# Small products of a token-mixing chain on four quarters of the matmul array, and a mean taken out of v beforehand

## The chip, the cores and the metric

The kernel runs on one core of a Trainium2 chip. The metric is device time in microseconds (us): the median of three runs, and beside it one execution taken by the hardware profiler. TensorE multiplies matrices, VectorE and ScalarE do elementwise work and copy results out of the accumulator memory (PSUM), GpSimd and SyncE mostly issue DMAs.

## The reference

A decoder trunk of two layers for one sequence of 512 tokens and 1,024 channels, in fp32. Each layer has three stages, each with an RMS norm, a shift, a scale and a gate made from a conditioning vector: a gated feed-forward net (width 2,816), a token mixing, and a second feed-forward net. The mixing projects the tokens to 20 tiles of 128 channels and runs three mixers on them: sliding-window attention with sinks, a short gated convolution, and the time mixing that this change is about:

```python
def step(S, inp):
    r_t, w_t, k_t, v_t, kk_t, a_t = inp
    s_kk = jnp.einsum('bhvk,bhk->bhv', S, kk_t)
    S = (S * w_t[:, :, None, :] - s_kk[..., None] * (kk_t * a_t)[:, :, None, :]
         + v_t[..., None] * k_t[:, :, None, :])
    return S, jnp.einsum('bhvk,bhk->bhv', S, r_t)
...
y = y - mean over the head;  y = y * rsqrt(var + eps) * gn_w + gn_b
```

It has four heads of 64 channels. Its decay w and its rate a come from low-rank products (64 inner channels each). y is linear in v, so the mean of y over a head's channels is zero when v's mean over them is taken out first.

## The kernel before, in words

All activations lie transposed: channels on the 128 partitions, the 512 tokens along the free dimension. Large products are done with each fp32 operand split into a rounded part H and a remainder L (`split`, L133 on ScalarE and L135 on VectorE), as three matmuls (`mm3`, L121 to L123). Feed-forward stages (`ffn`) stream weights and use the same three matmuls, at L420 to L422 for products of sums. Their moving operands are the normed activations hn (pools hnp and hnp2), combined halves com and hidden activations act (pool act). Pools are laid out one behind the other in on-chip memory; four tiles that are never used (shift, shift2, gap, gap2 of 448 and 64 bytes) move hnp, hnp2 and com against the rest.

`mix` (one call a layer) is written as Python generators that yield a cost. `products` emits the projection tiles and the first output products step by step; `attention` and two chains `rwkv(0)` and `rwkv(1)`, each for two heads, yield estimated costs. The loop at the end of `mix` emits product steps in proportion to those costs: RWKV_WORK, ATT_WORK and FILL_WORK are the totals, so a chain with a smaller total gets more product steps per unit of its cost. A scheduler then orders each engine's instructions; the order is fixed before the run, and an engine waits in it for what isn't ready.

A chain treats 512 tokens as 8 chunks of 64, that is 4 blocks b of two chunks c, and two heads e. Tiles [128, 2, 4, 64] hold chunk c on partition half c, with head e and block b along the free dimension. Its steps:

1. Low-rank products ps_w (L753) and ps_a (L755), contracting over the lower and the upper 64 partitions of lo and lw. lo has been through a tanh on ScalarE (L693).
2. Elementwise preparation on VectorE and ScalarE, with two reciprocals (L779, L780) and head sums by a block-of-ones matrix (`headsum`, L610).
3. `pairs` (L811): products of the chunks, ps_c, masked into B and K (L814).
4. The inverse of a unit triangular 64x64 matrix per chunk and head: its 16x16 diagonal blocks go through DRAM, are eliminated on VectorE (L839, L840) and come back as T and TT (L888, L889). Two levels of `each` (L897) join the blocks: ps_x, ps_t and ps_tt, with X (L902), T (L906) and TT (L909) taken out by one VectorE step of 512 columns each.
5. v, be and ka turned to token-major tiles by TensorE transposes (L853); values' share ps_xv (L874); W (ps_w2, L916; the profile names it ps_w), which multiplies TT into AX and is copied out negated (L917).
6. Per-chunk transfer ps_gn (L926 to L930), outputs ps_o (L942 to L946), six state steps ps_s (L954), their outputs ps_ys (L960).
7. Group norm: mean by `headsum` (ps_m), subtraction (L965), square, variance (ps_v), scale, bonus, gate (ps_g, L980).

A matmul takes its weights and moving operand from the partitions where they start and writes the partitions of its output, so an operand on 64 partitions and an output on 64 partitions use one quarter of the 128x128 array. In steps 4 and 5, chunk c reads partition half c and writes partition half c: two quarters on the diagonal. In ps_gn and ps_o, chunk c reads half c and head e writes half e, into one accumulator per c. Each chain owns two accumulator banks (tags r0 and r1).

## Time and profile before

| what | value |
|---|---|
| median of 3 runs | 1867.47 us (1863.78 to 1871.3) |
| the profiled execution | 1866.04 us, of which its span is 1864.0 |
| granted clock of TensorE | 0.994 |
| VectorE and ScalarE busy, share of the span | 75%, 45% |
| the two mixing stages | about 371 to 622 and 1285 to 1536 us of the span |

A group's row reads: line, engine, operation, output<-inputs, rows x columns of the array, shape, count; then busy us, mean ns of one; then idle time before it and what ended it. A timeline row reads: start, length, engine, line, operation, count of merged instructions. Matmuls overlap, so the distance between starts, and not the length of one, says how long a matmul holds the array. In the rows of waits stand the total, the number and the longest, in us.

### The profile page before, as it was taken

The page shows a single profiled execution, that of the slowest core. Times are in us where ns is not written, and L with a number is a line of the kernel's source. Part 1 is how long each engine was busy: PE and PEld are TensorE (multiplying, and loading weights), DVE is VectorE, ACT ScalarE, POOL GpSimd, SP SyncE. Part 2 cuts the span into 40 slices and gives each one's busy share as a digit, 9 for nine tenths or more (in the row PEclk, how much of TensorE's full clock was granted, in tenths as well). Part 3 has the DMA queues.
Part 4 walks back from the last instruction along what each step waited for, and adds up shares of the span by engine and source line. Part 5 has one row for each costly group of instructions (what it writes and reads, how often), then busy time and mean ns, then how long its engine had stood idle before and what let it go on. Part 6 is the DMA issues. An engine that isn't in the chain of part 4 may idle for free.

```text
span 1864.0 us, 33421 instructions
## 1 busy us (share of the span) xinstructions
PE 1828.7 (98%) x13664; PEld 1644.4 (88%) x13664; DVE 1398.4 (75%) x2202; ACT 836.3 (45%) x1272; POOL 130.9 (7%) x212
## 2 busy tenths in 40 slices
PE   8999999999999999999999999999999999999999
PEld 6889899986777999899999988999767788998998
DVE  7687677867986887777878786777589778874872
ACT  4443255346422555245345524544563335532551
POOL 0101110100000000110100020110000000100100
PEclk8999999999999999999999999999999999999999
DMA  7667876621122475886737688773212125775752
GB/s 307 225 185 234 263 197 202 221 83 46 58 55 72 136 195 176 296 223 195 246 112 197 171 272 228 192 229 114 101 56 59 53 68 161 209 227 139 203 144 68
DMA packets 104313, 308.24 MB, mean 165 GB/s; under 512 B 23392, under 2 KB 24416, under 8 KB 103136
## 3 DMA queue, kind: packets, MB, share of 16 engines
q1 hardware_dynamic: 75936, 203.34, 32.3%
q0 software_dynamic: 28224, 102.77, 21.7%
q8 instruction: 107, 1.75, 0.4%
q14 instruction: 46, 0.38, 0.1%
HBM read 302.66 MB, written 3.41 MB: 164 GB/s over the span
## 4 chain that ended last, share of the span: by engine, by line
PE 71%; DVE 13%; DMA 7%; issue 4%; ACT 4%; POOL 1%; SPq 0%; POOLq 0%; DVEq 0%; ACTq 0%
PE ps_mm L121 11%; PE ps_mm L122 10%; PE ps_mm L123 10%; PE ps_d L420 6%; PE ps_d L422 6%; PE ps_d L421 6%; PE ps_f L420 3%; PE ps_f L422 3%; PE ps_f L421 3%; DMA wada<-in_wadaT 2%; DVE wL L135 2%; PE ps_g L422 2%; PE ps_g L420 2%; PE ps_g L421 2%; ACT wH L133 1%
## 5 line engine op out<-in xcount | busy, mean ns | idle before, releaser
L133 ACT CAST wH<-wraw 128x1024 fp32r<-128x1024 f32 (+2 forms) x292 | 266.1, 918 | 434.7 <-PE ps_mm L122 190.2
L135 DVE TENSOR_TENSOR wL<-wraw,wH 128x1024 fp32r<-128x1024 f32 (+2 forms) x292 | 307.2, 1058 | 105.1 <-ACT wH L133 104.4
L123 PE MATMUL ps_mm<-actH,wL 128*128 128x512 f32 (+1 forms) x784 | 281.5, 359 | 2.8 <-DVE wL L135 2.8
L121 PE MATMUL ps_mm<-actH,wH 128*128 128x512 f32 (+1 forms) x784 | 281.6, 359 | 0.0
L122 PE MATMUL ps_mm<-actL,wH 128*128 128x512 f32 (+1 forms) x784 | 281.2, 359 | 0.0
L121 PE MATMUL ps_mm<-hnH,wH 128*128 128x512 f32 (+1 forms) x760 | 267.5, 359 | 5.7 <-ACT hnH L133 2.9
L122 PE MATMUL ps_mm<-hnL,wH 128*128 128x512 f32 (+1 forms) x760 | 266.5, 353 | 0.5
L123 PE MATMUL ps_mm<-hnH,wL 128*128 128x512 f32 (+1 forms) x760 | 266.4, 353 | 0.6 <-DVE wL L135 0.6
L420 PE MATMUL ps_d<-comH,wH 128*128 128x256 f32 x816 | 224.7, 275 | 0.3 <-ACT s L446 0.3
L421 PE MATMUL ps_d<-comL,wH 128*128 128x256 f32 x816 | 224.4, 275 | 0.0
L422 PE MATMUL ps_d<-comH,wL 128*128 128x256 f32 x816 | 224.4, 275 | 0.0
L192 DVE SCALAR_TENSOR_TENSOR wada<-wada,crep 128x1024 f32<-128x1024 f32 x140 | 167.7, 1219 | 48.8 <-DMA wada<-in_wadaT 48.2
L135 DVE TENSOR_TENSOR wL<-sum,wH 128x1024 fp32r<-128x1024 f32 x102 | 124.9, 1224 | 71.5 <-ACT wH L133 71.3
L123 PEld LDWEIGHTS ps_mm<-actH,wL 128*128 128x128 f32 x784 | 149.1, 190 | 20.3 <-DVE wL L135 3.6
L121 PEld LDWEIGHTS ps_mm<-hnH,wH 128*128 128x128 f32 x760 | 143.4, 191 | 24.9 <-issue 3.8
L121 PEld LDWEIGHTS ps_mm<-actH,wH 128*128 128x128 f32 x784 | 149.1, 190 | 16.8
L122 PEld LDWEIGHTS ps_mm<-actL,wH 128*128 128x128 f32 x784 | 149.0, 190 | 16.8
L123 PEld LDWEIGHTS ps_mm<-hnH,wL 128*128 128x128 f32 x760 | 145.5, 191 | 19.3 <-issue 4.3
L122 PEld LDWEIGHTS ps_mm<-hnL,wH 128*128 128x128 f32 x760 | 145.4, 192 | 17.2 <-DVE hnL L277 1.6
L420 PEld LDWEIGHTS ps_d<-comH,wH 128*128 128x128 f32 x816 | 156.7, 192 | 0.9 <-ACT s L446 0.9
L422 PEld LDWEIGHTS ps_d<-comH,wL 128*128 128x128 f32 x816 | 156.7, 192 | 0.0
L421 PEld LDWEIGHTS ps_d<-comL,wH 128*128 128x128 f32 x816 | 156.7, 192 | 0.0
(354 smaller groups left out, 3855.6 us busy)
## 6 DMA issues: line engine op xcount, KB each, us to landing
wada<-in_wadaT POOLq DMA_DIRECT2D x128, 512.0 KB, 4.8
wraw<-in_wmi SPq DMA_DIRECT2D x40, 512.0 KB
wraw<-in_w2p SPq DMA_DIRECT2D x36, 512.0 KB
wraw<-in_w1p SPq DMA_DIRECT2D x32, 512.0 KB
wraw<-in_w1o SPq DMA_DIRECT2D x32, 384.0 KB
wraw<-in_w2o SPq DMA_DIRECT2D x32, 384.0 KB
wraw<-in_w1i SPq DMA_DIRECT2D x20, 512.0 KB
wraw<-in_w1o SPq DMA_DIRECT2D x32, 320.0 KB
```

What stands on the lines that cost most here:

```text
L121: mm(acc, wH, xH, start=start, stop=False)
L122: mm(acc, wH, xL, start=False, stop=False)
L123: mm(acc, wL, xH, start=False, stop=stop)
L133: nc.scalar.copy(hi, src)
L135: return nc.vector.tensor_sub(lo, src, hi.bitcast(F32))
L192: stt(w, w, 1.0, crep, ALU.mult, ALU.mult, accum_out=out_)
L420: mm(acc, wH, xH, start=start and i + k == 0, stop=False, skip_group_check=True)
L421: mm(acc, wH, xL, start=False, stop=False, skip_group_check=True)
L422: mm(acc, wL, xH, start=False, stop=k == 3, skip_group_check=True)
```

## The change

- **Two quarters to four.** The products of the inverse, values' share and W write head 0's chunk c to partition half c of one accumulator (as before), and head 1's chunk c to half 1-c of a second. Each result is now copied out by three instructions: all of head 0, and the two halves of head 1, which change partition halves on the way. ps_t and ps_tt of the first level share a pair of accumulators; W is one block instead of two.
- **Low-rank products** are done in halves of 256 tokens, ps_w and ps_a in turn. They are ordered one behind the other across both chains, behind the tanh, and given high priority, so that all 16 follow each other.
- **Mean.** v is turned by a matmul against cen (identity minus the mean over a head) instead of a transpose. ps_m and its subtraction go. The bonus term uses the v that isn't centred. cen adds 128 columns (512 bytes a partition) to the constants.
- **Pads.** The four unused tiles go.
- **Order.** `pairs`, ps_gn and ps_o start with half 1 instead of half 0.
- **Planner.** The yields follow the shorter steps; RWKV_WORK is 24.3 instead of 29.8.

In the built programs each engine's order changes with it. On TensorE the 16 low-rank matmuls stand behind the second value product of attention's first block. Before the first chain's first ps_x stand 426 product matmuls of the stage (436 before) and 22 fewer of ps_c. VectorE's order has T ahead of both B steps, two convolution steps and a weight split, and ends the elimination ahead of the second reciprocal of the other chain.

```diff
-GAP = 448
-RWKV_WORK, ATT_WORK, FILL_WORK = 29.8, 15.2, 129.6
+RWKV_WORK, ATT_WORK, FILL_WORK = 24.3, 15.2, 129.6
...
-    ("ident", P), ("bones", P), ("bones2", 2), ("su", CH), ("iu", CH), ("diag", CH),
+    ("ident", P), ("bones", P), ("bones2", 2), ("cen", P), ("su", CH), ("iu", CH), ("diag", CH),
...
-    shift = ctx.enter_context(tc.tile_pool(name="shift", bufs=1))
-    shift.tile([P, GAP // 4], F32, name="shift")
     hnp = [ctx.enter_context(tc.tile_pool(name=n, bufs=KD)) for n in ("hnp", "hnp2")]
-    shift = ctx.enter_context(tc.tile_pool(name="shift2", bufs=1))
-    shift.tile([P, (512 - GAP) // 4], F32, name="shift2")
...
-            ap_.tile([P, GAP // 4], F32, name="gap", tag="gap")
-            ap_.tile([P, (512 - GAP) // 4], F32, name="gap2", tag="gap2")
...
-            act(got["lo"][:64], got["lo"][:64], AF.Tanh)
+            got["tanh"] = act(got["lo"][:64], got["lo"][:64], AF.Tanh)
...
             pw = psum([P, T], "ps_w", R)
-            mm(pw, lw[:64, cw], lo[:64], start=True, stop=True)
             pa = psum([P, T], "ps_a", R)
-            mm(pa, lw[64:, cw], lo[64:], start=True, stop=True)
-            yield 1.7
+            behind = got.get("lora", got["tanh"])
+            with tc.high_priority():
+                for sl in HALVES:
+                    for e, pt in enumerate((pw, pa)):
+                        m = mm(pt[:, sl], lw[rows[e], cw], lo[rows[e], sl], start=sl is HALVES[0], stop=sl is HALVES[1])
+                        tc.add_manual_dep(m.ins, behind.ins.name, ORDER, reason="halves of the rows run together")
+                        behind = got["lora"] = m
+            yield 1.2
...
-                        for e in range(2):
+                        for e in (1, 0):
                             mm(pts[e][rows[c], b], src[rows[e], n * CH : (n + 1) * CH], AR[rows[e], :, n], start=True, stop=True)
...
-                    nc.tensor.transpose(pt[:, b], src[:, b * P : (b + 1) * P], cst("ident"))
+                    x = src[:, b * P : (b + 1) * P]
+                    if name == "ps_vN":
+                        mm(pt[:, b], x, cst("cen"), start=True, stop=True)
+                    else:
+                        nc.tensor.transpose(pt[:, b], x, cst("ident"))
...
+            corners = [(b, e, c) for b in range(NB) for e, c in ((1, 1), (1, 0), (0, 1), (0, 0))]
+            def quarters(name, n=1, w=CH):
+                return [psum([P, n, NB, w], name, R) for _ in range(2)]
+            def gathered(pts, j):
+                return [(slice(0, P), 0, pts[0][:, j])] + [(rows[c], 1, pts[1][rows[1 - c], j]) for c in range(2)]
...
-            px = psum([P, 2, NB, CH], "ps_xv", R)
-            for e in range(2):
-                for b in range(NB):
-                    for c in range(2):
-                        mm(px[rows[c], e, b], K_[rows[c], e, b, 0], vN[rows[c], b, rows[e]], start=True, stop=True)
-            nc.scalar.copy(AX[:, :, :, 1], px)
-            yield 1.3
+            pts = quarters("ps_xv")
+            for b, e, c in corners:
+                mm(pts[e][rows[c ^ e], 0, b], K_[rows[c], e, b, 0], vN[rows[c], b, rows[e]], start=True, stop=True)
+            for r, e, x in gathered(pts, 0):
+                nc.scalar.copy(AX[r, e, :, 1], x)
+            yield 0.8
...
+            def each(pts, j, lhs, rhs):
+                for b, e, c in corners:
+                    mm(pts[e][rows[c ^ e], j, b], lhs[rows[c], e, b], rhs[rows[c], e, b], start=True, stop=True)
             for lev in range(2):
-                px = each("ps_x", LT, T_)
-                tt(X, px, rep2(f"lev{lev}", NB), ALU.mult)
-                yield 1.3
+                pts = quarters("ps_x")
+                each(pts, 0, LT, T_)
+                for r, e, x in gathered(pts, 0):
+                    tt(X[r, e], x, rep(f"lev{lev}", NB)[r], ALU.mult)
+                yield 0.8
+                pts = quarters("ps_t", 2 - lev)
                 if lev == 0:
-                    p1 = each("ps_t", TT, X)
-                    tt(T_, T_, p1, ALU.subtract)
-                    yield 1.3
-                p2 = each("ps_tt", X, TT)
-                tt(TT, TT, p2, ALU.subtract)
-                yield 1.3
+                    each(pts, 1, TT, X)
+                each(pts, 0, X, TT)
+                for j, to in ((1, T_), (0, TT))[lev:]:
+                    for r, e, x in gathered(pts, j):
+                        tt(to[r, e], to[r, e], x, ALU.subtract)
+                yield 1.4 - 0.6 * lev
...
-            for e in range(2):
-                pt = psum([P, NB, P], "ps_w2", R)
-                for b in range(NB):
-                    for c in range(2):
-                        mm(pt[rows[c], b], TT[rows[c], e, b], Wn[rows[c], e, b], start=True, stop=True)
-                nc.scalar.mul(Wn[:, e], pt, -1.0)
-                yield 1.1
+            pts = quarters("ps_w2", 1, P)
+            for b, e, c in corners:
+                mm(pts[e][rows[c ^ e], 0, b], TT[rows[c], e, b], Wn[rows[c], e, b], start=True, stop=True)
+            for r, e, x in gathered(pts, 0):
+                nc.scalar.mul(Wn[r, e], x, -1.0)
+            yield 1.3
...
-            ce = [(c, e) for c in range(2) for e in range(2)]
+            ce = [(c, e) for c in (1, 0) for e in (1, 0)]
...
-            pm = headsum(y, "ps_m", R)
-            stt(y, pm, -1.0 / CH, y, ALU.mult, ALU.add)
-            yield 0.9
...
-    con = [r == s, r // CH == s // CH, r // CH == np.arange(2)[None, :], u < v, u <= v]
+    con = [r == s, r // CH == s // CH, r // CH == np.arange(2)[None, :], (r == s) - (r // CH == s // CH) / CH, u < v, u <= v]
```

More of the change, by code (lines that the diff above doesn't have):

```diff
@@ L890, in rwkv @@
             X = S(q, "X", (P, 2, NB, CH))
-            def each(name, lhs, rhs):
-                pt = psum([P, 2, NB, CH], name, R)
-                for e in range(2):
-                    for b in range(NB):
-                        for c in range(2):
-                            mm(pt[rows[c], e, b], lhs[rows[c], e, b], rhs[rows[c], e, b], start=True, stop=True)
-                return pt
-            for lev in range(2):
-                px = each("ps_x", LT, T_)
-                tt(X, px, rep2(f"lev{lev}", NB), ALU.mult)
-                yield 1.3
-                if lev == 0:
-                    p1 = each("ps_t", TT, X)
-                    tt(T_, T_, p1, ALU.subtract)
-                    yield 1.3
-                p2 = each("ps_tt", X, TT)
-                tt(TT, TT, p2, ALU.subtract)
-                yield 1.3
@@ L911, in rwkv @@
-            Wn = AX.rearrange("p e b a t -> p e b (a t)")
-            for e in range(2):
-                pt = psum([P, NB, P], "ps_w2", R)
-                for b in range(NB):
-                    for c in range(2):
-                        mm(pt[rows[c], b], TT[rows[c], e, b], Wn[rows[c], e, b], start=True, stop=True)
-                nc.scalar.mul(Wn[:, e], pt, -1.0)
-                yield 1.1
+            def each(pts, j, lhs, rhs):
+                for b, e, c in corners:
+                    mm(pts[e][rows[c ^ e], j, b], lhs[rows[c], e, b], rhs[rows[c], e, b], start=True, stop=True)
```

## Prediction

> **What bounds the kernel now.** First the page's head and chain, then the busy time by window (columns: window, its length, busy us and count of TensorE matmul, weight load, VectorE, ScalarE, GpSimd, then granted clock, DMA share, GB/s), then TensorE's waits inside the first mixing stage.

> ```profile
> span 1864.0 us, 33421 instructions
> PE 1828.7 (98%) x13664; PEld 1644.4 (88%) x13664; DVE 1398.4 (75%) x2202; ACT 836.3 (45%) x1272; POOL 130.9 (7%) x212
> ...
> PE 71%; DVE 13%; DMA 7%; issue 4%; ACT 4%; POOL 1%; SPq 0%; POOLq 0%; DVEq 0%; ACTq 0%
> ```
> ```profile
> 371.00:622.00 251.00, 246.20 (x2172) 194.53 (x2171) 191.12 (x408) 111.76 (x231) 1.84 (x6) 1.00 0.20 62
> 1285.00:1536.00 251.00, 246.07 (x2169) 194.12 (x2167) 190.87 (x407) 111.69 (x231) 1.85 (x6) 1.00 0.21 62
> ...
> 440.00:480.00 40.00, 38.92 (x247) 24.84 (x248) 37.05 (x76) 23.33 (x53) 0.42 (x2) 1.00 0.19 54
> 480.00:520.00 40.00, 39.25 (x277) 30.91 (x277) 37.69 (x95) 15.77 (x35) 0.43 (x2) 1.00 0.19 60
> 520.00:560.00 40.00, 39.81 (x680) 31.47 (x678) 31.35 (x74) 12.49 (x22) 0.00 (x0) 1.00 0.17 45
> 560.00:600.00 40.00, 39.95 (x422) 31.64 (x419) 22.98 (x35) 9.05 (x13) 0.00 (x0) 1.00 0.26 84
> ```
> ```profile
> PE ps_pt L1041 <- DVE Sc L1029: 1.8, 3, 1.0
> ...
> PE ps_s L954 <- ACT y L949: 0.2, 1, 0.2
> ```

> The change lies in the mixing stages (the first two windows; the layers differ by 0.25 us of VectorE). TensorE is busy for 246 of 251 us, and its nine waits there (first and last shown) hold only a few us. So a microsecond taken from TensorE there is a microsecond of time, as long as nothing else becomes late. VectorE is the one to watch: 37 of 40 us until 520, with slack after (31 and 23 of 40), which is where the inverse and W stand.

> **The change, part by part.** Every fp32 matmul leaves two records. Now the small blocks:

> ```profile
> 543.18 1.02 PE L610 MATMUL ps_m<-y,con 128*128 128x512 f32 x2
> 544.13 1.15 PE L897 MATMUL ps_x<-T,B 64*64 64x64 f32 x32
> 545.21 0.48 PE L121 MATMUL ps_mm<-hnH,wH 128*128 128x512 f32 x1
> 545.53 0.38 PE L122 MATMUL ps_mm<-hnL,wH 128*128 128x512 f32 x1
> 545.74 0.38 PE L123 MATMUL ps_mm<-hnH,wL 128*128 128x512 f32 x1
> ```
> ```profile
> L897 PE MATMUL ps_x<-T,B 64*64 64x64 f32 x256 | 9.2, 221 | 0.0
> L916 PE MATMUL ps_w<-AX,TT 64*64 64x128 f32 x128 | 8.3, 274 | 0.0
> ```
> ```profile
> 565.30:567.60 2.30, 1.63 (x96) 1.49 (x96) 0.61 (x2) 1.00 0.12 21
> ```

> The last row is the window of ps_gn alone, whose matmuls already go to four quarters (row half c, column half e); ps_x uses the two diagonal ones. Less the one record that ends the block, ps_x takes (1.15-0.22)/31 = 0.030 us a record, ps_gn (1.63-0.22)/95 = 0.0148.

> *Inverse.* Five blocks of 32 records in each of two chains per layer: 31 x 0.0152 = 0.47 us a block, 2.35 a chain. Values' share (ps_xv): one such block, but the changed program's order issues it in pieces (3 and 13 matmuls in the first chain); I take half, 0.25.

> *W.* Two blocks of 16 records become one of 32:

> ```profile
> 559.22 1.09 PE L916 MATMUL ps_w<-AX,TT 64*64 64x128 f32 x16
> 560.24 0.48 PE L122 MATMUL ps_mm<-y5L,wH 128*128 128x512 f32 x1
> ```

> (1.09-0.27)/15 = 0.055 a record; no 128-wide block runs on four quarters, so I estimate the same factor, 0.027: 30 x 0.027 = 0.82 a chain (bounds: nothing, and 0.82). The block lost: it holds TensorE 1.02 until the next product, 0.14 over 16 records; 0.2 with its start.

> *Head mean.* ps_m goes: two records of 1.02-0.59 = 0.43, so 0.86 a chain, and one VectorE step. v's centring turns transposes of one record into matmuls of two:

> ```profile
> 521.31 0.66 PE L853 MATMUL ps_vN<-con,v 128*128 128x128 f32 x4
> ```

> Four more records of at most 0.66/4 = 0.16; less the last one's tail 0.13: +0.5 a chain.

> *Low-rank products.* Four blocks of two 512-wide records become one of 16 256-wide records, row halves in turn; attention's scores already run so:

> ```profile
> 442.88 1.12 PE L753 MATMUL ps_w<-lo,lw 64*128 64x512 f32 x2
> 443.93 0.66 PE L1041 MATMUL ps_pt<-con,Sc 128*128 128x128 f32 x4
> ```
> ```profile
> 449.14 1.13 PE L1001 MATMUL ps_sc<-kt,qr 64*128 64x256 f32 x8
> 450.21 0.48 PE L121 MATMUL ps_mm<-hnH,wH 128*128 128x512 f32 x1
> ```

> 4 x 1.05 = 4.2 plus 0.1 at each start; after, 1.07 x 2 = 2.1. Saved: 2.4 a layer. They move ahead, right behind attention's second value product, and wait for the tanh; behind them in the queue stand the next block's scores and all products.

> ```profile
> 427.64 1.49 PE L1059 MATMUL ps_av<-pmc,V 128*64 128x512 f32 x4
> ```
> ```profile
> 427.55 0.63 ACT L693 ACTIVATE lo<-lo 64x512 f32<-64x512 f32 x1
> ```

> The tanh ends at 428.18, inside the value product (until 429.1): no stall, with 0.9 us of cover.

> *Sum on TensorE.* 2.35 + 0.25 + 0.82 + 0.2 + 0.86 - 0.5 = 3.98 a chain, 7.96 a layer, with 2.4: 10.4 a layer, **20.7 us** in all. The reversed orders at L811 and in ps_gn and ps_o keep the same matmuls:

> ```profile
> 511.00:518.00 7.00, 3.79 (x64) 3.06 (x64) 1.27 (x2) 1.00 0.39 98
> ```

> 64 records of ps_c took 3.79. At 0.027 they would take 1.7; were the new order to bring that, 4 us a layer would go, and as little speaks for a loss of 1. I take nothing: the first records still wait for the same two VectorE steps.

> *What it costs.* Two accumulators cross-wise mean three copies out instead of one (128, 64 and 64 rows of 256):

> ```profile
> 518.49 0.67 DVE L902 TENSOR_TENSOR X<-ps_x,con 128x512 f32<-128x512 f32 x1
> 519.09 1.26 DVE L814 TENSOR_TENSOR K<-ps_c,con 128x512 f32<-128x512 f32 x2
> ```
> ```profile
> 530.54 0.41 DVE L932 TENSOR_TENSOR GT<-ps_gn,con 128x256 f32<-128x256 f32 x1
> 530.87 0.41 DVE L933 TENSOR_TENSOR N<-ps_gn,pc 128x256 f32<-128x256 f32 x1
> ```

> One 512-wide step holds VectorE for 0.60, a 256-wide one for 0.33: three make 1.0, +0.4; no row shows 64 rows that change halves, so bounds are 0.33 and 0.41 (no overlap). Five steps a chain: +2.0 VectorE, less 0.6 for the mean. VectorE's 191 of 251 can carry 2.8 more a layer, and ScalarE's 112 the extra copies of ps_xv and W. But each step is a link of a chain: the block before it is 0.47 shorter and the copy 0.4 longer, so products must cover 0.87 more, at five links in two chains 8.7 us a layer. In the changed order the products (0.21 each by the rows at 545.53 and 545.74) between links number 6, 3, 4 and 4 in the first chain, with other small blocks among them, and 21, 7, 0 and 5 in the second. Six cover 1.3 us, enough; three or four leave 0.4 to 0.8 open, none leaves 1.1. Together some 2 us in the first chain and 1.5 in the second: **3.5 a layer** of new waits. Bounds: 0 and 8.7.

> [...]

> The first chain must also not start late: TensorE reaches ps_x just as VectorE delivers T.

> ```profile
> 515.56 0.67 DVE L888 TENSOR_TENSOR T<-C,con 128x512 f32<-128x512 f32 x1
> ```
> ```profile
> 516.29 0.97 PE L897 MATMUL ps_x<-T,B 64*64 64x64 f32 x26
> ```

> In the changed order TensorE gets there with ten products and 22 small matmuls fewer, about 5.5 us sooner with the low-rank saving. VectorE's order puts T ahead of both B steps, two convolution steps and a weight split, and the elimination's last step ahead of the 3.3 us reciprocal: 4 to 5 us sooner too. I count no wait there.

> *Pads.* Without pads and with a 512-byte wider constant block, hn and com lie 64 bytes further on; the act tiles keep their place modulo 512.

> ```profile
> L122 PE MATMUL ps_mm<-actL,wH 128*128 128x256 f32 x160 | 44.0, 275 | 0.0
> L421 PE MATMUL ps_f<-hnL,wH 128*128 128x256 f32 x272 | 74.8, 275 | 0.0
> L421 PE MATMUL ps_d<-comL,wH 128*128 128x256 f32 x816 | 224.4, 275 | 0.0
> ```

> Shifted (hn, com) and unshifted (act) operands run alike: cost nothing.

> **Forecast.** 2 x (10.4 - 3.5) = 13.8 us off the profiled execution's 1866.04 (span 1864.0 and 2 around it) gives 1852.2; that execution is 1.4 below the median 1867.47, so the median comes to about **1853**.

> **Rivals.** *Two at a time.* If quarters of different row halves can't write one accumulator bank together, or a row half feeds one column half at a time, the blocks stay at 0.030: the inverse, ps_xv and W's 0.82 go (3.4 a chain), leaving 3.6 a layer against waits of about 2 (copies longer, blocks not shorter): 3 us, **1864**. For it: in ps_gn each bank belongs to one row half, here both halves share one. Against: ps_x shares a bank between two row halves and still runs two records at a time, since 64 columns alone would take 64/512 of ps_m's 0.43, 0.054. [...]

> *The chain takes the place.* All 8.7 us of lost cover turn into waits: 2 x 1.7 = 3.4 us, **1864**. For it: VectorE at 37 of 40 before 520, zero products at one link. Against: the slack after 520.

> *Slower: addresses.* If the 64 bytes set moving operands against weights, all matmuls on hn and com pay; the rows count at least 3 x 816 + 3 x 272 on com and hn alone, and L121 to L123 some 2,280 more: about 5,500. To lose 9.3 us in spite of 13.8 gained takes 23/5,500 = 4.2 ns each; 6 ns gives **1886**. The equal 275 ns speak against it.

> **How the numbers follow.** Half a per cent, 9.3 us, is about what can be told from no change. Forecast with waits of 0 to 5.5 a layer: 0.66 (1843 to 1858, faster). Two at a time 0.11 and the chain 0.13 (1858 to 1867, same). Addresses 0.10 (slower). The range leaves out the slower case and the ends: 1842 to 1867.

> **What would show it.** In the changed trace a 32-record block of ps_x or ps_t takes 0.7 us, not 1.15; the merged W 1.1 to 1.2; ps_m is absent; one low-rank block of 16 records takes 2 us; TensorE's new waits name X, T or TT on VectorE and hold 3 to 4 us a layer; the mixing windows shrink by 7 us each and the rest keeps its length. Blocks at 1.15, VectorE waits near 9 us a layer, or products on hn further apart than 0.22 us would make it wrong.

## The result, and the profile after

The changed kernel takes 1878.72 us (median of 8 runs, 1871.33 to 1886.17); the kernel before, beside it, 1867.87 us (median of 8). The ratio is **1.0062, with a 95% interval of 1.0043 to 1.0081: slower by 0.6%**, where 1853 us, faster, was forecast.

The head of the page after (span; busy time of each engine; the chain of waits by engine):

```profile
span 1876.6 us, 33525 instructions
...
PE 1820.6 (97%) x13688; PEld 1640.5 (87%) x13688; DVE 1409.5 (75%) x2238; ACT 839.7 (45%) x1284; POOL 131.2 (7%) x212
...
PE 65%; DVE 17%; DMA 9%; issue 5%; ACT 3%; POOL 1%; SPq 0%; DVEq 0%; POOLq 0%; ACTq 0%
```

TensorE is busy for 8 us less than before, and the span is 12.6 us longer: VectorE's share of the chain went from 13 to 17%. The mixing stages by window, from one norm's spread to the next (columns as in the prediction: window, length, TensorE's busy time, weight loads, VectorE, ScalarE, GpSimd, granted clock, DMA share, GB/s), before and then after:

```profile
369.30:614.10 244.80, 240.39 (x2129) 189.29 (x2128) 185.29 (x392) 106.54 (x221) 1.84 (x6) 1.00 0.20 60
1283.10:1527.70 244.60, 240.23 (x2128) 189.15 (x2127) 185.24 (x392) 106.52 (x221) 1.85 (x6) 1.00 0.20 60
```
```profile
366.50:615.50 249.00, 234.48 (x2131) 185.71 (x2131) 189.64 (x410) 108.36 (x227) 1.84 (x6) 0.97 0.19 59
1289.90:1540.20 250.30, 236.06 (x2130) 186.68 (x2130) 189.74 (x410) 108.56 (x227) 1.86 (x6) 0.97 0.20 59
```

Both stages grew, by 4.2 and 5.7 us, which is 9.9 of the span's 12.6. Two things are to be seen. TensorE's idle time (length less busy) went from 4.41 to 14.52 us in the first stage and from 4.37 to 14.24 in the second. And the granted clock is 0.97 in place of 1.00. The second is seen better in windows of 3.41 us, here of the changed kernel:

```profile
459.61:463.02 3.41, 1.99 (x33) 1.48 (x32) 3.41 (x8) 2.57 (x10) 0.00 (x0) 1.00 0.00 0
463.02:466.43 3.41, 3.15 (x19) 2.48 (x18) 3.06 (x8) 0.00 (x0) 0.00 (x0) 0.50 0.00 0
466.43:469.85 3.42, 3.42 (x15) 1.52 (x15) 2.89 (x6) 0.00 (x0) 0.00 (x0) 0.50 0.00 0
555.18:558.59 3.41, 1.36 (x32) 1.12 (x32) 3.29 (x7) 0.00 (x0) 0.00 (x0) 1.00 0.00 0
558.59:562.01 3.42, 2.33 (x35) 2.06 (x36) 3.30 (x8) 1.66 (x3) 0.00 (x0) 0.50 0.00 0
562.01:565.42 3.41, 3.41 (x36) 2.34 (x36) 3.38 (x6) 0.22 (x1) 0.00 (x0) 0.50 0.02 5
```

A window in which TensorE was busy for 1.99 or 1.36 us at full clock is followed by two at half clock. The first stage has these four, the second has five, and the mixing stages of the kernel before have none. At half clock the 512-wide products of the changed kernel start 0.42 and 0.43 us apart (561.34, 561.76 and 562.19), at full clock 0.21 to 0.22 (565.56, 565.77 and 565.99). If all the work done in the four (3.15 + 3.42 + 2.33 + 3.41 = 12.31 us) took half as long at full clock, they cost up to 6.2 us; the sum row of the second stage's five:

```profile
sum 17.06, PE 16.39 PEld 11.05 DVE 15.63 ACT 3.29 POOL 0.00; mean PE 3.28 PEld 2.21 DVE 3.13 ACT 0.66 POOL 0.00
```

which is up to 8.2 us. So the balance of a stage, in us, is as follows. Its first row counts all work at half clock as half as long, so it is an estimate at the upper end:

| | layer 0 | layer 1 |
|---|---|---|
| matmul time at full clock | 240.4 to 228.3: -12.1 | 240.2 to 227.9: -12.4 |
| TensorE idle | +10.1 | +9.9 |
| half clock, at most | +6.2 | +8.2 |
| length of the stage | +4.2 | +5.7 |

TensorE's waits in the first mixing stage (columns: us in total, times, longest), new or grown ones:

```profile
PE ps_x L904 <- DVE TT L918: 3.5, 2, 1.8
PE ps_t L904 <- DVE X L910: 3.3, 3, 2.2
...
PE ps_o L950 <- DVE N L941: 1.5, 1, 1.5
PE ps_c L809 <- DVE a L795: 1.4, 1, 1.4
...
PE ps_w L923 <- DVE TT L918: 0.6, 1, 0.6
```

They name the links of the inverse, as the prediction said they would; but they hold some 9 us, not 3 to 4, and ps_c's wait for a is a new one elsewhere.

What the half clock really costs can be read where the same instructions ran with different numbers of half-clock windows. In all traced kernels with the low-rank products ahead, and in both layers, the same 90 TensorE records run from the first chain's bonus product (458.72 us in the changed kernel) to the last of its ps_c (472.95):

| half-clock windows in it | stages | us from start to start |
|---|---|---|
| 0 | 5 | 12.1 |
| 1 | 1 | 12.55 |
| 2 | 7 | 14.1 to 14.5 |
| 3 | 3 | 15.25 to 15.6 |

The changed kernel took 14.23 us there in the first layer and 15.31 in the second, so 2.1 and 3.2 us were lost to the clock at this place.

### The profile page after: what moved, and what is told of

Its sections match the earlier page's. It is cut to its first block, busy times and chain, and to the rows that moved or that the text cites. A ratio compares the mean times of both kernels' runs of the same rounds, so it can differ in the third digit from the quotient of the medians.

```text
span 1876.6 us, 33525 instructions
## 1 busy us (share of the span) xinstructions
PE 1820.6 (97%) x13688; PEld 1640.5 (87%) x13688; DVE 1409.5 (75%) x2238; ACT 839.7 (45%) x1284; POOL 131.2 (7%) x212
## 3 DMA queue, kind: packets, MB, share of 16 engines
q8 instruction: 107, 1.75, 0.4%
HBM read 302.72 MB, written 3.41 MB: 163 GB/s over the span
## 4 chain that ended last, share of the span: by engine, by line
PE 65%; DVE 17%; DMA 9%; issue 5%; ACT 3%; POOL 1%; SPq 0%; DVEq 0%; POOLq 0%; ACTq 0%
PE ps_mm L116 9%; PE ps_mm L117 9%; PE ps_mm L118 9%; PE ps_d L413 6%; PE ps_d L415 6%; PE ps_d L414 6%; DMA wada<-in_wadaT 3%; PE ps_f L413 3%; PE ps_f L415 3%; PE ps_f L414 3%; DVE wL L130 2%; PE ps_g L415 2%; PE ps_g L413 2%; PE ps_g L414 2%; DVE wada L187 2%
```

## The experiments

Each ratio is to the kernel before, run beside it. "Clock" is the mean granted clock of the timed runs; that of the kernel before is 0.995, that of the changed kernel 0.986.

**Quarters out.** The changed kernel with the inverse, W and the values' share as before:

```
-  pts = quarters("ps_x"); each(pts, 0, LT, T_)       # and ps_t, ps_xv, ps_w2
-  for r, e, x in gathered(pts, 0): tt(X[r, e], x, ...)
+  px = each("ps_x", LT, T_)
+  tt(X, px, rep2(f"lev{lev}", NB), ALU.mult)
```

> The changed kernel, with inverse, values' share and W put back on two quarters with one step out each (the rest of the change stays: low-rank products in row halves, v centred, no pads). Link theory (the three-step copies of the inverse and the few products between its links make TensorE wait, and those waits bring half-clock windows): the waits on X, T, TT and N go (some 9 us a layer), low-rank and mean keep their 6 us, so 1858 to 1866. If the early wait for ps_c at 461 us (with two to three half-clock windows behind it) comes from the earlier low-rank products, it stays and the time is 1866 to 1872. Address theory (missing pads): no gain, 1876 or more.

Measured: 1865.59 us, ratio **0.9973 (0.9956 to 0.9991)**, clock 0.992.

```profile
365.90:607.80 241.90, 234.54 (x2132) 188.25 (x2131) 182.76 (x390) 106.44 (x221) 1.83 (x6) 1.00 0.20 61
1280.40:1523.40 243.00, 236.70 (x2131) 189.57 (x2130) 182.96 (x390) 106.68 (x221) 1.85 (x6) 0.99 0.19 60
```

The first stage saves 5.9 us of busy time and pays 2.9 of it in idle time (7.36 against 4.41). This is the fastest kernel of the study, a little faster than both: without the quarters the change gains.

**Quarters alone.** The kernel before, with those three parts on quarters and nothing else:

> The kernel before, with only the inverse, the values' share and W on four quarters (work budget 25.7 to fit). Link theory: 14.5 us of matmul time saved, some 18 us of waits on X, T, TT and N in the two layers and four half-clock windows of up to 1.7 us each added: 1872 to 1882. Address theory: the pads are still there, so only the saving shows: 1853 to 1862.

Measured: 1876.57 us, ratio 1.0047 (1.0029 to 1.0066), clock 0.993: the slowdown comes with the quarters, pads or not.

```profile
367.00:614.80 247.80, 235.49 (x2119) 183.09 (x2118) 190.88 (x412) 108.90 (x227) 1.83 (x6) 0.99 0.19 59
```

Idle time is 12.3 us, 7.9 more than before.

**Pads out.** The kernel before without `shift`, `shift2`, `gap` and `gap2`:

> The kernel before without its four pads and nothing else (hn and com lie 64 bytes further on modulo 512, as in the changed kernel). Link theory: nothing, 1864 to 1872. Address theory: slower by all that the change lost, 1880 or more.

Measured: 1871.26 us, ratio 1.0005 (0.9984 to 1.0026). The rival of the addresses falls.

**Three copies, two quarters.** The kernel before, each copy of the inverse cut in three:

```
-  tt(X, px, rep2(f"lev{lev}", NB), ALU.mult)          # and T_, TT
+  for r, e in ((slice(0, P), 0), (rows[0], 1), (rows[1], 1)):
+      tt(X[r, e], px[r, e], rep(f"lev{lev}", NB)[r], ALU.mult)
```

> The kernel before, with each copy of the inverse made in three pieces (128, 64 and 64 rows of 256) in place of one, matmuls on two quarters as before: VectorE gets 0.65 x 5 x 2 = 6.5 us a layer more, TensorE nothing. If the longer copy alone makes the waits: 6 us a layer and half-clock windows behind, 1880 or more. If the links of the kernel before still cover it with their products: 0 to 3 us a layer, 1868 to 1875.

Measured: 1877.61 us, ratio 1.0050 (1.0032 to 1.0068), clock 0.994.

```profile
368.40:617.30 248.90, 242.21 (x2128) 189.88 (x2128) 191.04 (x412) 106.28 (x221) 1.84 (x6) 1.00 0.20 59
```

Without one matmul fewer and at full clock, longer copies alone cost 4.1 us a stage (2.3 idle, 1.8 of busy time, with VectorE's at 191 in place of 185). The time lies between the two expectations, so neither holds.

**Idle matmuls in many waits.** The changed kernel, with matmuls on constants whose result nobody reads:

```
+  def fill(n, behind):
+      pf = psum([P, T], "ps_fill")
+      for _ in range(n):
+          m = mm(pf, ones_r, wide, start=True, stop=True)   # ordered behind `behind`
```

> The changed kernel with idle matmuls (one record of 512 columns each, on constants, into an accumulator that nobody reads) right behind the blocks whose successors wait: 3, 8 and 7 of them in the first chain of a layer, 3, 7 and 7 in the second, 35 x 0.215 = 7.5 us a layer. Clock theory (a wait lowers the busy share of one 3.41 us window and the next two run at half clock): the half-clock windows behind the second chain go, the waits are filled, and the time falls by 2 to 8 us, to 1871 to 1877. If the waits alone are the loss and the clock costs nothing: 1878 to 1881. If there is no room for them: up to 15 us slower, 1894.

Measured: 1878.53 us, ratio 1.0055 (1.0033 to 1.0078), clock 0.992. The clock theory's range is missed; the time lies in that of the rival, by which half clock costs nothing. In the first stage the half-clock windows are gone, yet it is as long:

```profile
368.80:617.60 248.80, 238.43 (x2167) 188.84 (x2166) 188.97 (x410) 108.73 (x227) 1.83 (x6) 1.00 0.19 59
```

Idle time fell by only 4.1 us (14.52 to 10.37) for 7.5 us of idle matmuls, so they outgrew the waits. This run can't tell what the clock gave: with so many of them, the order of VectorE's, ScalarE's and TensorE's other instructions changed too.

**Idle matmuls in two waits.** The same with four behind the ps_t block and four behind the second ps_x block of the second chain alone:

> The changed kernel with eight idle matmuls a layer (1.7 us), in the second chain alone: four behind the ps_t block and four behind the second ps_x block, where TensorE waits 1.85 and 2.35 us. TensorE's work between grows by less than the wait, so it costs nothing by itself. Clock theory: the window in which TensorE was busy for 1.36 of 3.41 us rises to some 3 us, the two half-clock windows behind it go, 2 to 3 us a layer less, 1872 to 1876. If half clock costs nothing there: 1877 to 1880.

Measured: 1871.25 us, ratio **1.0016 (0.9996 to 1.0035)**, clock 0.993, against the changed kernel's 1.0062. The same stretch, by windows and on TensorE's timeline (start, us, engine and line, operation, in brackets the wait before it):

```profile
555.01:558.42 3.41, 2.44 (x37) 1.79 (x36) 3.27 (x8) 1.01 (x2) 0.00 (x0) 1.00 0.00 0
558.42:561.84 3.42, 2.59 (x40) 1.56 (x38) 3.32 (x7) 1.31 (x3) 0.00 (x0) 1.00 0.00 0
```
```profile
551.70 0.69 PE L914 MATMUL ps_t<-X,TT 64*64 64x64 f32 x32 [0.92 <-DVE X L922]
...
552.80 1.20 PE L749 MATMUL ps_fill<-ones_r 128*128 128x512 f32 x4
556.25 0.68 PE L914 MATMUL ps_x<-T,B 64*64 64x64 f32 x16 [0.97 <-DVE TT L931]
...
557.89 1.20 PE L749 MATMUL ps_fill<-ones_r 128*128 128x512 f32 x4
559.92 0.69 PE L914 MATMUL ps_t<-TT,X 64*64 64x64 f32 x32 [0.83 <-DVE X L922]
```

The waits left (0.92 + 0.97 + 0.83 = 2.72) and eight idle matmuls (1.7) are together as long as the three waits of the changed kernel (0.55 + 1.68 + 2.19 = 4.42, rows below): nothing got earlier. But TensorE was busy for 2.44 us in the window and not for 1.36, and the clock stayed at 1.00. VectorE's and ScalarE's instructions stand in the same order in both kernels. From the second chain's first ps_x to its first ps_gn it now takes 20.8 and 21.0 us in the two layers; in the changed kernel, with two windows at half clock each, 22.3 and 22.5. So here matmuls that compute nothing made the kernel faster, by 1.5 us a layer, and the half clock is a cause of its own.

The rest of the gain is not theirs, as far as this trace goes. The mixing stages of this execution:

```profile
364.10:613.80 249.70, 237.21 (x2140) 187.10 (x2139) 189.75 (x410) 108.50 (x227) 1.83 (x6) 0.97 0.20 59
1285.90:1532.50 246.60, 232.92 (x2139) 184.85 (x2138) 189.55 (x410) 108.48 (x227) 1.84 (x6) 0.99 0.20 60
```

The first is no shorter than the changed kernel's 249.0: three half-clock windows stand behind ps_c's wait for a and one at 517. The second, with one, is 3.7 us shorter; 2.8 of that were saved behind ps_c's wait (12.55 in place of 15.31), where no idle matmul stands. Together that is 3.0 of the 7.5 us by which the spans differ; 4.5 lie outside the mixing stages, where nothing was changed. So it is not shown that the idle matmuls gave more than 1.5 us a layer.

**Copies first.** The changed kernel with the inverse's copies at high priority, so that their three pieces stand together:

```
+  with tc.high_priority():
       for r, e, x in gathered(pts, 0):
           tt(X[r, e], x, rep(f"lev{lev}", NB)[r], ALU.mult)      # and T_, TT
```

> The changed kernel, with the inverse's copies issued ahead of other VectorE work: in the second chain the three pieces of a copy then stand next to each other (in the changed kernel steps of y and of the convolution stand between them). If the waits come from that tearing: the waits on X and TT in the second chain shrink by 1.5 to 2.5 us a layer, its half-clock windows go, 1870 to 1875. If they come from the length of three steps and from missing products: 1877 to 1880.

Measured: 1873.68 us, ratio 1.0035 (1.0020 to 1.0050), clock 0.992.

```profile
366.00:612.80 246.80, 231.59 (x2131) 183.07 (x2130) 189.67 (x410) 108.32 (x227) 1.83 (x6) 0.99 0.20 59
```

The time is that expected, the reason is not: TensorE idles for 15.2 us, no less than the 14.5 of the changed kernel. But the longest wait on X is 0.6 and no longer 2.2 us (that on TT stays at 1.8), and one window ran at half clock and not four. So the tearing set where TensorE waits, not how long in all.

**Both.** Copies first and idle matmuls in the two waits:

> The changed kernel with both: the inverse's copies ahead of other VectorE work, and four idle matmuls behind the ps_t block and the second ps_x block of the second chain. If the copies' place and the clock are two losses that add: 1866 to 1871. If the idle matmuls only hid the waits that the copies' place has removed already: like the copies alone, 1872 to 1875.

Measured: 1869.95 us, ratio 1.0017 (0.9997 to 1.0037), clock 0.993. The time lies in the range of the two that add, but the kernel before took only 1865.49 beside it, and by ratio it is no better than the idle matmuls alone (1.0016). From the second chain's first ps_x to its first ps_gn it takes 20.4 us, where the copies first alone took 21.0 and the idle matmuls alone 20.8 and 21.0: both remove the same two half-clock windows, and hardly add. What is left at half clock, three windows and two, stands behind ps_c's wait for a.

**W and the values' share on quarters, the inverse not:**

> The changed kernel with the inverse alone on two quarters with one step out; W and the values' share stay on four, whose copies are ScalarE's. If only the inverse's links on VectorE cost: 5 us less than the variant without any of the quarters (1866), 1859 to 1863, and faster than the kernel before. If ScalarE's copies in three pieces wait in the same way: 1865 to 1870.

Measured: 1866.29 us, ratio 0.9997 (0.9979 to 1.0015), clock 0.992; not the 1859 to 1863 of the first theory, but in the lower half of the other theory's range. It can't be told from the kernel before, while the changed kernel's 1.0062 can: most of the loss comes with the inverse's quarters. ScalarE's copy of W, 0.60 us in one step in the variant without quarters, takes 1.80 in three here: 1.2 us more on the link to ps_gn, and later TensorE waits 1.5 us for y from ScalarE where it waited 0.5:

```profile
PE ps_s L963 <- ACT y L958: 1.5, 1, 1.5
```

**Centring alone**, in the kernel before (without pads):

> The kernel before, without pads, with v centred when it is turned and no mean product (work budget 28.9), nothing else. By the prediction's rows: 0.86 off and 0.5 on in each chain, 0.36 x 4 = 1.4 us off, and one VectorE step of 0.6 per chain: 1863 to 1868. If all that the variant without quarters won (5 us) came from the centring: 1861 or less.

Measured: 1867.67 us, ratio 1.0004 (0.9989 to 1.0019). No gain that can be told.

**Low-rank products not ahead**, in the variant without quarters (`tc.high_priority()` and the link to the tanh removed):

> The variant without any of the quarters (1865.6), with the low-rank products in alternating row halves, but issued where they stood before (the second chain's then lie between the products for the bonus and ps_c). Theory: their move ahead bared the wait of ps_c for a at 461 us (1.4 us a layer and now and then half-clock windows behind it), so the wait falls under 0.5 us, and the time is 1860 to 1864, the fastest so far. Rival: the move ahead is what saves (TensorE never reaches the tanh late): 1866 to 1870.

Measured: 1868.39 us, ratio 1.0006 (0.9988 to 1.0023). My theory that the move ahead only bared a wait falls: the wait of ps_c for a shrank from 1.4 to 0.4 us, but ps_o waits in both layers, 1.8 us each, where the variant without quarters had no wait:

```profile
PE ps_o L944 <- DVE N L935: 3.7, 2, 1.8
```

**Low-rank products alone**, in the kernel before:

> The kernel before with the low-rank products alone changed (alternating row halves, ahead, right behind attention's second value product; work budget 29.3), pads and all else as before. By the prediction's rows 2.4 us a layer off: 1861 to 1863, if the baseline is 1866; the wait of ps_c for a and now and then half-clock windows behind it come with it, so up to 1865. If the variant without the quarters (0.9973) owed its gain to the combination with the centring: 1866 to 1868.

Measured: 1870.02 us, ratio 1.0008 (0.9991 to 1.0024). No gain either, and slower than all that was expected:

```profile
365.40:609.70 244.30, 236.93 (x2128) 188.19 (x2127) 184.08 (x392) 106.25 (x221) 1.83 (x6) 1.00 0.20 60
```

3.5 us of busy time saved, 3.0 of idle time added (7.37). With the centring and the other order as well, the idle time is the same 7.36 (first experiment) while 5.9 us are saved. This fits a new wait that is paid once, behind which further savings count; no run shows it by itself.

## Why the prediction was wrong, point by point

*Matmul time: right, if anything too small.* 10.4 us a layer were forecast, and TensorE's work shrank by some 12, an upper estimate. Part of that is not the forecast's: without the quarters, 5.9 us went in the first layer, where the forecast's rows give 2.4 for the low-rank products and 2 x 0.36 for the mean, 3.1 together. The blocks of the changed kernel on TensorE's timeline:

```profile
426.24 0.48 PE L751 MATMUL ps_w<-lo,lw 64*128 64x256 f32 x1
...
427.86 0.38 PE L751 MATMUL ps_a<-lo,lw 64*128 64x256 f32 x1
...
525.00 1.10 PE L923 MATMUL ps_w<-AX,TT 64*64 64x128 f32 x32 [0.62 <-DVE TT L918]
...
545.50 0.69 PE L904 MATMUL ps_x<-T,B 64*64 64x64 f32 x32
...
551.47 0.69 PE L904 MATMUL ps_t<-X,TT 64*64 64x64 f32 x32 [0.55 <-DVE X L910]
556.02 1.48 PE L904 MATMUL ps_x<-T,B 64*64 64x64 f32 x32 [1.68 <-DVE TT L918]
559.68 1.13 PE L904 MATMUL ps_t<-TT,X 64*64 64x64 f32 x32 [2.19 <-DVE X L910]
```

ps_x takes 0.69 (0.7 forecast), W 1.10 (1.1 to 1.2), the low-rank block from 426.24 to 428.24, 2.0 us (2.0). "Two at a time" falls with it: quarters of both row halves write one accumulator bank, and the records come (0.69 - 0.22)/31 = 0.015 us apart. The last two rows show what went wrong: a wait of 1.68 and one of 2.19, and blocks of 1.48 and 1.13 us in place of 0.69, one torn, the other at half clock.

*The step that failed: "3.5 a layer of new waits".* Idle time grew by 10 us a layer: some 9 at the links, above all on X and TT, 1.4 at ps_c and 0.5 at the bonus, less 1.0 of waits that went. Three sizes were off, and one link was not in the sum at all. First, the copy. VectorE in the changed kernel:

```profile
548.74 0.36 DVE L910 TENSOR_TENSOR X<-ps_x,con 128x256 f32<-128x256 f32 x1
549.01 0.74 DVE L978 SCALAR_TENSOR_TENSOR y<-y,par,gnrs 128x512 f32<-128x512 f32 x1
549.79 0.43 DVE L910 TENSOR_TENSOR X<-ps_x,con 64x256 f32<-64x256 f32 x1
550.13 0.74 DVE L979 SCALAR_TENSOR_TENSOR y<-y,par,bonus 128x512 f32<-128x512 f32 x1
550.90 0.42 DVE L910 TENSOR_TENSOR X<-ps_x,con 64x256 f32<-64x256 f32 x1
...
554.16 1.28 DVE L918 TENSOR_TENSOR T<-T,ps_t 128x256 f32<-128x256 f32 x3
555.45 1.31 DVE L918 TENSOR_TENSOR TT<-TT,ps_t 128x256 f32<-128x256 f32 x3
```

Three pieces hold VectorE for 1.29 us (554.16 to 555.45), 0.43 each, without overlap: 0.7 more than one step of 0.60, not 0.4. I had taken the lower of two bounds, 0.33 a piece; the measured 0.43 is above the upper one, 0.41. Second, the pieces aren't one after another: in the second chain two steps of y stand between those of X, and the last piece ends 2.6 us after the first began. By the run with copies first this decides where TensorE waits, but not how long in all. Third, one place was not looked at. Before, between the bonus and ps_c, TensorE had the second chain's low-rank product:

```profile
462.82 1.13 PE L610 MATMUL ps_bo<-bonus,con 128*128 128x512 f32 x2
463.87 1.12 PE L755 MATMUL ps_a<-lo,lw 64*128 64x512 f32 x2
465.09 1.76 PE L811 MATMUL ps_c<-AR,a 64*64 64x128 f32 x32
```
```profile
458.72 1.12 PE L603 MATMUL ps_bo<-bonus,con 128*128 128x512 f32 x2 [0.49 <-DVE bonus L786]
461.27 1.76 PE L809 MATMUL ps_c<-AR,a 64*64 64x128 f32 x32 [1.42 <-DVE a L795]
```

The prediction asked whether the moved products stall where they go to, and not what they had covered where they came from.

The link that was not in the sum is the one that the list of waits names ps_x on TT. ps_x reads T and B, not TT. In the kernel before, the second ps_x started 0.15 us after T was copied, ahead of TT's copy:

```profile
551.36 0.63 DVE L906 TENSOR_TENSOR T<-T,ps_t 128x512 f32<-128x512 f32 x1
552.56 0.68 DVE L909 TENSOR_TENSOR TT<-TT,ps_tt 128x512 f32<-128x512 f32 x1
```
```profile
552.14 1.15 PE L897 MATMUL ps_x<-T,B 64*64 64x64 f32 x32
```

In the changed kernel T is copied at 555.44, but ps_x starts at 556.02, 0.15 us after the first piece of TT's copy, and its last 16 records start behind that copy's last piece, from 556.81 to 557.27 (the 1.48 us in the row above). By T alone the last could start at 555.44 + 0.15 + 31 x 0.015 = 556.06, so this costs some 1.2 us, an estimate; in the first chain the same reckoning gives 1.5. The reason is most likely the accumulators: a chain has two, a block on quarters takes both, so the next block must wait until both are copied out. A run with more accumulators for a chain would show it; there is none.

*The rival "The chain takes the place"* had the size of the waits (8.7 a layer), and still not the time: it gave 1864.

*What no step held: the clock.* The sums were made at full clock. In the profiled execution half clock cost 2.1 and 3.2 us behind ps_c's wait, and 1.5 and 1.6 in the second chain (against the run with idle matmuls in two waits): 3.6 and 4.8 us of the 4.2 and 5.7 by which the stages grew. So the new waits ate what the matmuls had saved, and of the 9.9 us of slowdown beyond that 8.4 are half clock. Of these, 5.3 stand behind the wait that came with the low-rank products, and not with the quarters. The mean clocks of the timed runs fit roughly: if work at half clock takes twice as long (0.42 to 0.43 us in place of 0.21 to 0.22 for a product), half clock costs at most (1 - clock) of the time, 0.014 x 1879 = 26 us after and 0.005 x 1868 = 9 before. If six tenths of the difference are lost, as in the trace (8.4 of at most 14.4), that is 10 us, and the changed kernel would be at about 1869 without it, an estimate: no slower than before, but not the forecast's gain. The prediction's own windows had clock 1.00 everywhere, and it never asked what keeps it there.

*Pads:* right, no cost. *"The rest keeps its length":* right within 3 us (1377.3 against 1374.6).

## What to carry to other kernels

A matmul packed tighter paid here only as far as its successor's copy kept up (blocks of 0.69 us in place of 1.15, copies of 1.29 in place of 0.60, and with the quarters alone a ratio of 1.0047): count the copy's pieces at their full length, without overlap (0.43 us each here), look who is issued between them (two steps of y, 0.74 us each), and count the accumulators that the block now takes (that they set the start of ps_x was not shown). Where products are moved ahead, price what they covered at the old place (ps_c then waited 1.42 us for a). And where TensorE is the bound, look at the busy share of each short window as well as at the sum. Here waits of 1.68 and 2.19 us cost more than their length, another 1.5 us, as two windows at half clock followed. The idle time spread out (copies first: 15.2 us of it in a stage of 246.8, against 14.5 in 249.0), or filled with matmuls that compute nothing (1.5 us a layer less), was cheaper.

## What the runs showed of the hardware

| busy in 3.41 us | windows | next one at half clock |
|---|---|---|
| under 1.63 us (48%) | 26 | 26 |
| 1.63 to 2.2 us | 91 | 26 |
| over 2.2, under 2.9 us | 213 | 1 |

In the first 40 us it was otherwise: there all 28 windows at full clock with TensorE busy for under 2.9 us were followed by half clock (2.29 and 2.78 us in the kernel before, 2.40 and 2.81 in the changed one); the reason is open. In the changed kernel two waits of 1.68 and 2.19 us in neighbouring links were enough: they left TensorE busy for 1.36 us of the window from 555.18 to 558.59, and half clock followed. Where the grid falls differs from execution to execution, and from layer to layer within one (in the changed kernel half clock begins 1.75 us after the first record of ps_c behind the wait for a in the first layer, at 463.02, and 0.05 before it in the second, at 1384.62): behind the same wait for a, between none and three windows ran at half clock.
